# Second feed-forward block of a macaron block: its input half by Strassen's product with seven half-depth products, its output half in three chunks of rows

## The chip, the cores and the metric

The kernel runs on one core of one Trainium2 chip. The metric is the time of one execution on the device in microseconds (us). Three runs of the kernel before gave 2293.59, 2286.38 and 2290.88 us, so the median is 2290.88 us. One execution was profiled; all times of single instructions come from it.

## The reference

A block of a streaming encoder works on x with 1024 tokens of 1024 features:

```python
x = x + 0.5 * swiglu_ffn(rms_norm(x, ffn1_norm), ffn1_w_in, ffn1_w_out)
h = rms_norm(x, mix_norm)
...                                  # three mixers on h, merged by gates, times w_out, added to x
x = x + 0.5 * swiglu_ffn(rms_norm(x, ffn2_norm), ffn2_w_in, ffn2_w_out)
x = rms_norm(x, final_norm)

def swiglu_ffn(h, w_in, w_out):
    gate, up = split(h @ w_in, 2)    # w_in [1024, 2 * 2816], w_out [2816, 1024]
    return (silu(gate) * up) @ w_out
```

Only the second feed-forward block, the hand-over to it and the end of the kernel are touched by the change.

## The kernel before, in words

Every large product is computed from two fp16 parts of each operand, hi and lo, with three matmuls per 128 rows of depth: hi·hi, hi·lo and lo·hi (`matmul3`). A matmul has 128 output features on the partitions and 512 tokens, one half of the sequence, in its columns.

**Input half** (`ffn_in`). It has 22 tiles f. A tile is 128 gate columns and 128 up columns of w_in, for both halves of the tokens: 2 halves × 2 × 8 depths × 3 = 96 matmuls, 2112 for all. The gate's sum lies in PSUM as `mm`, the up one's as `lg`. ScalarE takes silu of the gate (`si`), and VectorE multiplies (`gt`). `Rows.put` then makes row f of the matrix for the output half: ScalarE squares `gt` for a sum, VectorE gets a power of two from it (`rsc`, `Hi`, `Hj`), ScalarE makes the hi part of `H` and VectorE the lo part.

**Weights** (`WBlock`). A block is loaded by a DMA (`wf`, two buffers), squared on ScalarE, summed over the partitions by a small matmul with ones (`ms`), turned into a scale on VectorE (`wsc`), and split: hi on ScalarE, lo on VectorE (`wh`, three buffers).

**Output half** (`out_stage`, blocks from `out_block`). There are 16 units: 8 tiles d of 128 output features by two halves. A unit is 22 rows × 3 = 66 matmuls: 60 for the first 20 rows in a bank `mm` (`begun`) and 6 for the last two rows in a bank `lg` (`ended`), since the scales of the weights' rows depend on the rows of H (`wrs`). VectorE adds both to x (`xo`, `xn`). In `final` the result is transposed, squared and normalized: on the last tile d = 7 a chain of twelve small operations on VectorE (`nv`, `ny`, `rsu`) gives 1/rms, and the 128x1024 tiles are scaled and stored. `tail_order` puts the last m tiles d half by half, here m = 2: (6,0), (7,0), (6,1), (7,1). The last unit comes in two pieces of 256 tokens.

**The hand-over.** The stage ahead multiplies the merged mixers by w_out. When a half of x is complete, `norm_split` scales it by 1/rms and the gain on VectorE (`hs<-xa,gs,lg`), copies hi on ScalarE (`xa<-hs`), and subtracts for lo on VectorE and GpSimd in turn (`xa<-hs,xa`). The input half begins with half 0 of two tiles, so 96 matmuls need nothing of half 1.

**What sets the order.** The program is written by generators under one clock model: `Model` estimates each engine's time, `Sched` lets the thread go on that is due, and `Stream.prep` emits the steps of the weight blocks ahead of their use when their engines are at most 3 us behind TensorE. Each engine then executes its own instructions in this order, waiting where an operand is not there. All instructions pass one helper, so the profile shows the line L61 for each, and groups are told apart by the tiles' names.

## Time and profile before

| | |
|---|---|
| median of three runs | 2290.88 us (2286.38 to 2293.59) |
| profiled execution, span | 2287.5 us |
| profiled execution's own time beside its span | not listed by itself; the runs' median is 3.4 us above the span |
| PE, DVE, ACT, POOL busy | 96%, 55%, 51%, 10% of the span |
| matmul instructions | 12604 |
| first product of the second input half | starts at 1574.53 us |
| first product of its output half | starts at 2039.92 us |

PE is TensorE, DVE VectorE, ACT ScalarE and POOL GpSimd. The busy shares are means over stages which differ: in the second feed-forward block GpSimd does nothing and the other two are busy for about a third of the time.

### The profile page before, as it was taken

The numbers are of one execution on the slowest core, as the hardware profiler recorded it, in microseconds if no ns is written. First come the engines' busy times: TensorE is split into PE (matmuls) and PEld (weight loads), VectorE is DVE, ScalarE is ACT, GpSimd is POOL, SyncE is SP. The second block draws the span as 40 slices with busy tenths as digits, with TensorE's granted clock in tenths as the row PEclk, the third lists the DMA queues.
The fourth block names the chain that finished last, engine by engine and source line by source line (L and its number), as shares of the span: only waits on it lengthen the run. The fifth ranks groups of instructions, "written<-read, shape, count | busy, mean of one in ns | idle before, by whom it ended". The sixth has DMA issues, their size and how long they took to land.

```text
span 2287.5 us, 33499 instructions
## 1 busy us (share of the span) xinstructions
PE 2192.5 (96%) x12604; PEld 1146.7 (50%) x12604; DVE 1258.8 (55%) x3818; ACT 1163.3 (51%) x2471; POOL 220.9 (10%) x463
## 2 busy tenths in 40 slices
PE   6999999999999889989999999899999999999998
PEld 3555444444444556575566764344444444444445
DVE  6446843244554477768569877667332233245553
ACT  6543434344443588778876766535343334344331
POOL 1201130000000013302200015401000000000000
PEclk9999999999999999989999999999999999999999
DMA  6422231202232111214322123353111111212212
GB/s 221 126 80 79 58 102 56 62 26 84 92 107 65 42 38 61 78 30 147 102 70 70 48 89 116 100 156 107 56 40 53 56 56 37 70 44 69 70 41 87
DMA packets 210866, 176.79 MB, mean 77 GB/s; under 512 B 7008, under 2 KB 187424, under 8 KB 210064
## 3 DMA queue, kind: packets, MB, share of 16 engines
q1 hardware_dynamic: 195008, 131.64, 18.4%
q0 software_dynamic: 8272, 28.84, 4.0%
q10 hardware_dynamic: 7424, 14.18, 2.1%
q8 instruction: 98, 1.61, 0.3%
q14 instruction: 64, 0.52, 0.1%
HBM read 139.38 MB, written 36.30 MB: 77 GB/s over the span
## 4 chain that ended last, share of the span: by engine, by line
PE 71%; DVE 13%; ACT 9%; issue 3%; POOL 2%; DMA 1%; DVEq 0%; ACTq 0%; POOLq 0%
PE mm L61 44%; PE lg L61 24%; ACT junk L61 3%; PE ms L61 3%; DVE at L61 2%; DVE wh L61 2%; DVE xa L61 1%; DVE dump L61 1%; PE ao L61 1%; ACT wh L61 1%; DVE wk L61 1%; DVE sb L61 1%; ACT mp L61 1%; POOL rsu L61 1%; DVE hs L61 1%
## 5 line engine op out<-in xcount | busy, mean ns | idle before, releaser
L61 PEld LDWEIGHTS <-wh 128*128 128x128 f16 x8418 | 816.5, 98 | 988.6 <-issue 35.9
L61 PE MATMUL mm<-xa,wh 128*128 128x512 f16 x3264 | 735.2, 380 | 6.4 <-ACT xa L61 4.9
L61 PE MATMUL lg<-xa,wh 128*128 128x512 f16 x2112 | 476.3, 380 | 0.0
L61 DVE SCALAR_TENSOR_TENSOR gt<-lg,wsc,si 128x512 f32<-128x512 f32 x88 | 66.0, 750 | 367.7 <-PE lg L61 346.7
L61 PE MATMUL mm<-H,wh 128*128 128x512 f16 (+1 forms) x1020 | 213.0, 366 | 0.0
L61 PE MATMUL mm<-G,wh 128*128 128x512 f16 x960 | 210.5, 379 | 0.0
L61 ACT ACTIVATE junk<-wf 128x128 f16<-128x128 f32 (+3 forms) x332 | 200.9, 605 | 17.9 <-DMA wf<-in_w_in_dram 10.5
L61 DVE SCALAR_TENSOR_TENSOR wh<-wf,wsc,wh 128x1024 f16<-128x1024 f32 (+1 forms) x132 | 166.1, 1261 | 56.5 <-ACT wh L61 56.4
L61 ACT ACTIVATE wh<-wf,wrs 128x128 f16<-128x128 f32 (+2 forms) x392 | 130.4, 403 | 103.9 <-DVE wrs L61 103.9
L61 ACT ACTIVATE si<-mm,wsc 128x512 f32<-128x512 f32 x88 | 59.7, 678 | 218.1 <-PE mm L61 207.6
L61 ACT ACTIVATE junk<-gt 128x1024 f16<-128x1024 f32 x44 | 46.5, 1056 | 237.7 <-DVE gt L61 237.7
L61 ACT ACTIVATE wh<-wf,wsc 128x1024 f16<-128x1024 f32 (+1 forms) x132 | 147.1, 1120 | 18.8 <-DVE wsc L61 17.2
L61 PE MATMUL mm<-wh,xa 128*128 128x256 f16 (+2 forms) x1152 | 130.8, 273 | 12.2 <-ACT us L61 6.6
L61 DVE SCALAR_TENSOR_TENSOR wh<-wf,wrs,wh 128x128 f16<-128x128 f32 (+2 forms) x392 | 124.8, 373 | 15.9 <-ACT wh L61 14.7
L61 PEld LDWEIGHTS <-xa 128*128 128x128 f16 x1152 | 108.7, 107 | 31.0 <-issue 13.8
L61 ACT ACTIVATE junk<-wk,kathr 128x1024 f16<-128x1024 f32 (+2 forms) x96 | 99.5, 1036 | 8.7 <-POOL kathr L61 6.8
L61 POOL TENSOR_TENSOR xa<-hs,xa 128x512 f16<-128x512 f32 x24 | 29.2, 1218 | 585.6 <-ACT xa L61 585.6
L61 DVE SCALAR_TENSOR_TENSOR xo<-mm,wsc,xo 128x512 f32<-128x512 f32 (+1 forms) x33 | 24.2, 734 | 92.2 <-PE mm L61 90.2
L61 ACT ACTIVATE sq<-xa 128x512 f32<-128x512 f32 x28 | 17.6, 629 | 109.0 <-DVE xa L61 105.7
L61 DVE TENSOR_SCALAR_CACHE_REDUCE dump<-wk,kt 128x384 f16<-128x384 f32 (+2 forms) x96 | 71.3, 743 | 2.0
L61 PE MATMUL mm<-m,wh 128*128 128x512 f16 x288 | 68.5, 393 | 3.7 <-DVE wh L61 3.2
L61 ACT ACTIVATE at<-at,asm,gac 128x128 f32<-128x128 f32 (+7 forms) x64 | 55.3, 865 | 27.3 <-DVE asm L61 26.9
(479 smaller groups left out, 2431.7 us busy)
## 6 DMA issues: line engine op xcount, KB each, us to landing
wf<-in_ffn_w_in_dram SPq DMA_DIRECT2D x88, 512.0 KB, 4.6
wf<-in_ffn_w_out_dram SPq DMA_DIRECT2D x16, 1280.0 KB, 6.0
gd<-gt SPq DMA_DIRECT2D x48, 256.0 KB, 2.0
xa<-gd POOLq DMA_DIRECT2D x16, 768.0 KB, 5.0
wf<-in_w_in_dram SPq DMA_DIRECT2D x17, 512.0 KB, 4.8
xo<-xd ACTq DMA_DIRECT2D x32, 256.0 KB, 2.6
xd<-xa SPq DMA_DIRECT2D x32, 256.0 KB, 2.4
wf<-in_w_in_dram SPq DMA_DIRECT2D x8, 1024.0 KB, 5.0
```

The lines of the kernel that those rows point to most:

```text
L61: r = f(*a, **k)
```

## The change

The product [gate; up] = w_inᵀ h is cut into 2 × 2 × 2: gate or up columns, the two halves of the depth, the two halves of the tokens. Strassen's product (in Winograd's form) then needs seven products of half the depth in place of eight. Per tile these are A11·B11, A12·B21, S1·T1, S2·T2, S3·T3, A22·T4 and S4·B22: 7 × 4 depths × 3 = 84 matmuls.

- **Sums of weights** (`SBlock`): four additions of 128x512 on GpSimd give S1 to S4 in one buffer `wsum`. Seven forms of 512 columns are split to hi and lo, in two buffers of the ring: A11, A12, S1, S2, and A22, S3, S4.
- **Sums of h** (`norm_forms` in place of `norm_split`): B11 and B21 from half 0 alone, then T2, T1, T3, T4 and B22, for which half 1 is needed; subtractions on VectorE and GpSimd, hi copies on ScalarE, lo on VectorE.
- **Sums of products** (`ffn_strassen`): ScalarE copies A11·B11 out of PSUM (`s["a"]`), VectorE makes five additions, each with one operand in PSUM, and GpSimd both products with silu. Their results lie in the place of x (names `xa` and `early`).
- **Output half**: rows 0 to 7 are multiplied after tile 8 of the input half, rows 8 to 14 after tile 15, rows 15 to 21 at the end. A chunk uses blocks of 256 columns. The first two chunks add to x in DRAM (`xd`): a unit reads its tile, VectorE adds, SyncE's queue writes it back. The last chunk is `out_stage` with `per` = 2 and m = 1.

```diff
+class SBlock(WBlock):
...
+        add = lambda o, x, y, op: nc.gpsimd.tensor_tensor(o, x, y, op=op)
+        if i == 0:
+            add(s1, self.a(2), self.a(3), OP.add)
+            add(s2, s1, self.a(0), OP.subtract)
+        else:
+            add(s3, self.a(0), self.a(2), OP.subtract)
+            add(s4, self.a(1), s2, OP.subtract)
...
+    def norm_forms(self, xa, half, sums, gi, name, F):
...
+        for k in range(K):
+            norm(k)
+            sub(nc.gpsimd, h(k, 0), h(k, 1), h(k, 0))
+            norm(k + K)
+            yield pace()
+        for k in range(K):
+            t2 = sp(self.t2("hs"))
+            sub(nc.vector, t2, h(k + K, 1), h(k, 0))
+            parts("T2", k, t2, nc.vector)
+            sub(nc.gpsimd, h(k + K, 0), h(k + K, 0), t2)
+            yield pace()
...
+                if form == "T3":
+                    sub(nc.gpsimd, h(k, 1), h(k + K, 1), h(k, 1))
+                parts(form, k, src(k), nc.vector)
...
+    def ffn_strassen(self, name, rows, a, b, F, ring, chunks, xd):
...
+            product(b2, w, "S2", "T2", False)
+            u2, u3 = ring(), ring()
+            nc.vector.tensor_tensor(u2, b2, s["a"], op=OP.add)
...
+            product(b3, w, "S1", "T1", False)
...
+            product(b2, w, "S3", "T3", True)
+            nc.vector.tensor_tensor(u3, b2, s["a"], op=OP.add)
...
+            nc.vector.tensor_tensor(c22, b3, u3, op=OP.add)
+            product(b4, w, "A22", "T4", False)
+            nc.vector.tensor_tensor(u3, b4, u3, op=OP.add)
+            gt = st[f] = ring("gt")
+            nc.gpsimd.tensor_tensor(gt[:, 0:HT], u3, s["si"], op=OP.mult)
...
+            product(b3, w, "S4", "B22", True)
+            w.use[1].uses -= 1
+            nc.vector.tensor_tensor(u2, b3, u2, op=OP.add)
+            nc.scalar.activation(u2, u2, AF.Silu, scale=w.inv)
+            nc.gpsimd.tensor_tensor(gt[:, HT:2 * HT], c22, u2, op=OP.mult)
...
+        yield f"h{name}.0"
+        for f in range(2):
+            yield from head1(f)
+        for f in range(2):
+            yield from head2(f)
+        for f in range(2):
+            yield from body(f, "f" + name + ".{}" if f == 0 else None, False)
+            put(f)
...
-    g1, g2 = Rows(kb, NF, "G"), Rows(kb, NF, "H")
+    chunks = [(0, 8), (8, 15), (15, 22)]
...
-            yield from kb.out_stage(b2, g2, xo, xd[2], 1, 2, done, cut=(0, HT // 2, HT), between=between)
+            yield from kb.out_stage(b2[-1], g2, xo, xd[2], 2, 1, done, cut=(0, HT // 2, HT), between=between)
```

The clock model orders the program anew, so the engines' orders move. On VectorE between two tiles of the input half, the order before is as follows (`wsc` the next weights' scale, `gt` the products with silu, `rsc` to `H` the row, `wh` the low parts of the next weights):

```order
L61 TENSOR_SCALAR wsc_18235<-wsc_18235,ginv_102 128x1
L61 SCALAR_TENSOR_TENSOR gt_18254<-lg_18185,wsc_17824,si_18255 128x512
L61 SCALAR_TENSOR_TENSOR gt_18254<-lg_18259,wsc_17824,si_18308 128x512
L61 TENSOR_SCALAR rsc_18311<-rsc_18311 128x1 x2
L61 TENSOR_SCALAR Hi_105<-rsc_18311 128x1
L61 TENSOR_TENSOR Hj_106<-Hi_105 128x1
L61 SCALAR_TENSOR_TENSOR H_18312<-gt_18254,rsc_18311,H_18312 128x1024
L61 SCALAR_TENSOR_TENSOR wh_18335<-wf_18201,wsc_18235,wh_18335 128x1024 x2
```

After the change the same place reads as follows (`xa<-lg` and `xa<-ao` are the additions of products; `wsum` holds S1 and S2 in the first of its splits, S3 and S4 in the second):

```order
L61 TENSOR_SCALAR wsc_17195<-wsc_17195,ginv_102 128x1
L61 TENSOR_TENSOR xa_91<-ao_17130,xa_91 128x512
L61 TENSOR_TENSOR xa_91<-lg_17202,xa_91 128x512
L61 SCALAR_TENSOR_TENSOR wh_17218<-wf_17009,wsc_17195,wh_17218 128x1024
L61 TENSOR_TENSOR xa_91<-ao_17130,xa_91 128x512
L61 SCALAR_TENSOR_TENSOR wh_17218<-wsum_17144,wsc_17195,wh_17218 128x1024
L61 TENSOR_SCALAR rsc_17238<-rsc_17238 128x1 x2
L61 TENSOR_SCALAR Hi_105<-rsc_17238,wsc_17057 128x1
L61 TENSOR_TENSOR Hj_106<-Hi_105 128x1
L61 SCALAR_TENSOR_TENSOR H_17239<-xa_91,rsc_17238,H_17239 128x1024
```

The low parts of S1 and S2 of the next tile now stand behind the last addition of this tile (`xa<-ao`), ahead of the row's chain; before, the next weights' low parts stood behind the row.

On VectorE at the hand-over, for half 1 of h, the order before is (a part of the eight pairs):

```order
L61 SCALAR_TENSOR_TENSOR hs_16316<-xa_91,gs_177,lg_16291 128x512
L61 SCALAR_TENSOR_TENSOR hs_16318<-xa_91,gs_177,lg_16291 128x512
L61 TENSOR_TENSOR xa_91<-hs_16316,xa_91 128x512
L61 SCALAR_TENSOR_TENSOR hs_16322<-xa_91,gs_177,lg_16291 128x512
L61 SCALAR_TENSOR_TENSOR hs_16326<-xa_91,gs_177,lg_16291 128x512
L61 TENSOR_TENSOR xa_91<-hs_16322,xa_91 128x512
L61 SCALAR_TENSOR_TENSOR hs_16330<-xa_91,gs_177,lg_16291 128x512
L61 SCALAR_TENSOR_TENSOR hs_16348<-xa_91,gs_177,lg_16291 128x512
```

After the change it is (`FT2`, `FT1` and `FT3` are the low parts of forms of h, `hs` the difference T2 itself, `early` a sum of products of the first tile):

```order
L61 SCALAR_TENSOR_TENSOR xa_91<-xa_91,gs_177,lg_16263 128x2x256 x8
L61 TENSOR_TENSOR hs_16307<-xa_91 128x512
L61 TENSOR_TENSOR FT2_15407<-hs_16307,FT2_15407 128x512
L61 TENSOR_TENSOR hs_16312<-xa_91 128x512
L61 TENSOR_TENSOR FT2_15407<-hs_16312,FT2_15407 128x512
L61 TENSOR_TENSOR hs_16317<-xa_91 128x512
L61 TENSOR_TENSOR FT2_15407<-hs_16317,FT2_15407 128x512
L61 TENSOR_TENSOR hs_16322<-xa_91 128x512
L61 TENSOR_TENSOR FT2_15407<-hs_16322,FT2_15407 128x512
L61 TENSOR_TENSOR FT1_15408<-xa_91,FT1_15408 128x512 x4
L61 TENSOR_TENSOR FT3_15409<-xa_91,FT3_15409 128x512
L61 TENSOR_TENSOR early_16352<-lg_16338,early_16201 128x512
```

All eight norms now come ahead of the first form, and five forms of four pieces follow them (T4 and B22 come behind the rows shown); before, each piece of h was ready for TensorE after its own norm and subtraction.

At the start of the last chunk of the output half, VectorE has after the change (`wrs` the scales of its rows 15 to 19, `H_20533` row 21):

```order
L61 TENSOR_TENSOR xa_91<-ao_20414,xa_91 128x512
L61 TENSOR_SCALAR wsc_20520<-ms_20521 128x1
L61 TENSOR_SCALAR wsc_20520<-wsc_20520 128x1 x2
L61 TENSOR_SCALAR wrs_20526<-Hi_105,wsc_20520 128x5
L61 SCALAR_TENSOR_TENSOR junk2_20530,wrq_20500<-wf_20428 128x256
L61 TENSOR_SCALAR rsc_20532<-rsc_20532 128x1 x2
L61 TENSOR_SCALAR Hi_105<-rsc_20532,wsc_20335 128x1
L61 TENSOR_TENSOR Hj_106<-Hi_105 128x1
L61 SCALAR_TENSOR_TENSOR H_20533<-xa_91,rsc_20532,H_20533 128x1024
L61 SCALAR_TENSOR_TENSOR wh_20546<-wf_20287,wrs_20526,wh_20546 128x256 x5
L61 SCALAR_TENSOR_TENSOR wj_20564,wss_20475<-wrq_20476,Hj_106 128x2
```

where before it had:

```order
L61 TENSOR_SCALAR wrs_19337<-Hi_105,wsc_19331 128x20
L61 SCALAR_TENSOR_TENSOR wh_19351<-wf_19056,wrs_19337,wh_19351 128x128 x8
L61 SCALAR_TENSOR_TENSOR gt_19305<-lg_19316,wsc_18783,si_19392 128x512
L61 TENSOR_SCALAR rsc_19395<-rsc_19395 128x1 x2
L61 TENSOR_SCALAR Hi_105<-rsc_19395 128x1
L61 TENSOR_TENSOR Hj_106<-Hi_105 128x1
L61 SCALAR_TENSOR_TENSOR H_19396<-gt_19305,rsc_19395,H_19396 128x1024
L61 SCALAR_TENSOR_TENSOR wh_19351<-wf_19056,wrs_19337,wh_19351 128x128 x4
```

Before, the first eight low parts of the output weights stood ahead of the last row's chain; now all five of the chunk's first block stand behind it.

## Rows read from the trace of the kernel before

**Rows 1.** The page: busy time and share of each engine, and two lines of the span in 40 slices (tenths busy; PEclk is TensorE's granted clock in tenths).

```profile
PE 2192.5 (96%) x12604; PEld 1146.7 (50%) x12604; DVE 1258.8 (55%) x3818; ACT 1163.3 (51%) x2471; POOL 220.9 (10%) x463
PE   6999999999999889989999999899999999999998
PEclk9999999999999999989999999999999999999999
```

**Rows 2.** Busy time of each engine in stretches (from:to, length, then PE, PEld, DVE, ACT, POOL busy with counts, then TensorE's granted clock, the DMA engines' share and GB/s).

```profile
1550.00:1574.00 24.00, 20.98 (x104) 10.07 (x103) 18.47 (x38) 11.19 (x17) 3.65 (x4) 1.00 0.33 100
1650.00:1700.00 50.00, 49.90 (x236) 22.70 (x235) 14.38 (x29) 16.55 (x25) 0.00 (x0) 1.00 0.22 64
2200.00:2250.00 50.00, 50.00 (x246) 24.02 (x245) 20.07 (x65) 11.02 (x37) 0.00 (x0) 1.00 0.06 17
```

**Rows 3.** The order of time (start, us, engine, operation): three half tiles of the input half and the start of the output half.

```profile
2014.00 5.34 PE L61 MATMUL lg<-xa,wh 128*128 128x512 f16 x24
2019.18 5.34 PE L61 MATMUL mm<-xa,wh 128*128 128x512 f16 x24
2024.36 5.34 PE L61 MATMUL lg<-xa,wh 128*128 128x512 f16 x24
...
2039.92 7.93 PE L61 MATMUL mm<-H,wh 128*128 128x512 f16 x36
```

**Rows 4.** Groups of instructions from 1600 to 2030 us, by tile and shape (count, busy us, mean ns, idle before).

```profile
L61 DVE SCALAR_TENSOR_TENSOR wh<-wf,wsc,wh 128x1024 f16<-128x1024 f32 x38 | 48.6, 1281 | 10.9 <-ACT wh L61 10.9
L61 ACT ACTIVATE wh<-wf,wsc 128x1024 f16<-128x1024 f32 x38 | 43.0, 1133 | 0.0
L61 ACT ACTIVATE junk<-wf 128x1024 f16<-128x1024 f32 x36 | 37.5, 1041 | 0.0
...
L61 ACT ACTIVATE si<-mm,wsc 128x512 f32<-128x512 f32 x42 | 28.4, 677 | 137.1 <-PE mm L61 137.1
L61 DVE SCALAR_TENSOR_TENSOR H<-gt,rsc,H 128x1024 f16<-128x1024 f32 x21 | 27.0, 1284 | 20.2 <-ACT H L61 20.2
...
L61 ACT ACTIVATE junk<-gt 128x1024 f16<-128x1024 f32 x21 | 22.2, 1056 | 111.9 <-DVE gt L61 111.9
```

**Rows 5.** Operations of 128x512 with both operands in SBUF on GpSimd and VectorE in the order of time, alone (the first two) and beside each other.

```profile
1362.04 1.26 POOL L61 TENSOR_TENSOR sb<-sb,sm 128x512 f32<-128x512 f32 x1 [7.12 <-DMA wf<-in_w_glu_dram]
1363.51 0.69 DVE L61 SCALAR_TENSOR_TENSOR xa<-xa 128x512 f32<-128x512 f32 x1 [1.55 <-ACT xa L61]
...
1377.54 1.28 DVE L61 SCALAR_TENSOR_TENSOR m<-xa,rsc,m 128x1024 f16<-128x1024 f32 x1
1377.72 2.23 POOL L61 TENSOR_TENSOR sb<-sb,sm 128x512 f32<-128x512 f32 x1 [4.86 <-DVE sm L61]
1378.74 1.76 DVE L61 SCALAR_TENSOR_TENSOR xa<-xa 128x512 f32<-128x512 f32 x1
```

**Rows 6.** The hand-over in the order of time: pieces of h for half 0, the first product, half 1's first pieces.

```profile
1566.32 1.29 ACT L61 ACTIVATE xa<-hs 128x512 f16<-128x512 f32 x2 [2.01 <-DVE hs L61]
1566.98 0.69 DVE L61 TENSOR_TENSOR xa<-hs,xa 128x512 f16<-128x512 f32 x1
...
1567.59 1.40 DVE L61 SCALAR_TENSOR_TENSOR hs<-xa,gs,lg 128x512 f32<-128x512 f32 x2
1567.69 1.16 POOL L61 TENSOR_TENSOR xa<-hs,xa 128x512 f16<-128x512 f32 x1 [84.83 <-ACT xa L61]
...
1574.53 0.82 PE L61 MATMUL mm<-xa,wh 128*128 128x512 f16 x3
...
1592.20 1.40 DVE L61 SCALAR_TENSOR_TENSOR hs<-xa,gs,lg 128x512 f32<-128x512 f32 x2
```

**Rows 7.** Short stretches around waits of TensorE, columns as in rows 2.

```profile
1579.00:1583.00 4.00, 1.75 (x14) 1.09 (x11) 2.41 (x5) 3.28 (x6) 0.00 (x0) 1.00 0.24 79
1583.00:1587.00 4.00, 4.00 (x14) 1.75 (x14) 3.02 (x13) 3.97 (x4) 0.00 (x0) 0.57 0.83 248
```

**Rows 8.** The last row's chain at the start of the output half, in the order of time.

```profile
2040.20 0.75 DVE L61 SCALAR_TENSOR_TENSOR gt<-lg,wsc,si 128x512 f32<-128x512 f32 x1 [4.35 <-PE lg L61]
...
2043.72 1.28 DVE L61 SCALAR_TENSOR_TENSOR H<-gt,rsc,H 128x1024 f16<-128x1024 f32 x1 [0.96 <-ACT H L61]
2044.92 1.13 DVE L61 SCALAR_TENSOR_TENSOR wh<-wf,wrs,wh 128x128 f16<-128x128 f32 x4
```

**Rows 9.** The end of the kernel in the order of time: the first rms chain's scalings, unit (6,1)'s last matmuls, the last unit in two pieces, the last rms chain.

```profile
2252.31 0.69 DVE L61 TENSOR_TENSOR xa<-lg,gb 128x512 f32<-128x512 f32 x1 [5.17 <-ACT junk L61]
...
2255.29 2.08 DVE L61 TENSOR_SCALAR xa<-xa,ny 128x1024 f32<-128x1024 f32 x3
...
2259.58 1.46 PE L61 MATMUL lg<-H,wh 128*128 128x512 f16 x6
2260.87 2.13 PE L61 MATMUL mm<-H,wh 128*128 128x256 f16 x18
...
2276.19 0.82 PE L61 MATMUL lg<-H,wh 128*128 128x256 f16 x6
...
2281.68 0.75 DVE L61 TENSOR_SCALAR xa<-xa,ny 128x1024 f32<-128x1024 f32 x1
```

## Prediction made before the changed kernel was run

> **What bounds the kernel now.** I read the page first, then the stretches, then the order of time at four places. TensorE is busy for 96% of the span at its full granted clock; GpSimd for 10% [rows 1]. By stretches the stages differ: around the hand-over TensorE works 21.0 of 24 us with VectorE busy for 18.5, while in the middle of the second feed-forward block it works 49.9 of 50 us in the input half and 50.0 in the output half, with VectorE and ScalarE busy for a third or less and GpSimd not at all [rows 2]. So matmuls taken from that block come off the end one for one, as long as no operand comes later than TensorE asks for it. The question is how many such waits the change makes.
>
> The sum is made against the profiled span, 2287.5 us; the median of the runs, 2290.88, is 3.4 above, and I add these at the end.
>
> **Term 1, the matmuls: −57.0.** A half tile of 24 matmuls starts 5.18 us after the one before (2014.00, 2019.18, 2024.36), so one takes 0.2158 us [rows 3]. Twelve fewer in each of 22 tiles are 264, worth 57.0 us. The output half has 1056 before and after: 8 + 7 + 7 rows are the same 22.
>
> **What lies beside them.** A tile now lasts 84 × 0.2158 = 18.1 us. VectorE has five additions of some 0.69, seven forms of low parts (3584 columns at 1.281 per 1024: 4.5), the row's low part 1.28 and small ones for about 1.4: 10.6. ScalarE has one copy and two silus (0.68 each), hi parts (3584 columns at 1.133 per 1024: 4.0), squares of weights about 2.5 (2 × 1.04 and the sums' reads), and the row (1.06 and about 1.3): some 10.9 [rows 4]. GpSimd's six operations at 1.2 make about 7.3 [rows 5]. None of the three fills the tile, so no engine becomes the bound by its load and this work costs nothing as long as the order suits. In the first two chunks a unit of 24 or 21 matmuls lasts 4.5 to 5.2 us; its addition on VectorE is 0.75 and its read and write of 256 KB lie behind TensorE, so I take 0 (upper end +4, should one read in each chunk come late).
>
> Where GpSimd and VectorE meet, rows 5 show a price: an operation of 1.26 on GpSimd took 2.23 and one of 0.69 on VectorE took 1.76 when both read two tiles in SBUF. In rows 6, where VectorE's operation has an operand in PSUM (`hs<-xa,gs,lg`, two in 1.40), it loses nothing beside GpSimd's 1.16. The Trainium skill, "SBUF — State Buffer", section "Who interferes with whom", says the same: a VectorE instruction with at most one SBUF input does not contend with GpSimd, one with two contends with its reads. By that rule a tile's five additions, each with an operand in PSUM, would pay nothing, and only splits and forms would; the trace agrees as far as it goes.
>
> **Term 2, the start of the input half: +29.** Count from the first product on h (1574.53 before). Before, 2112 matmuls took until 2039.92, 465.4 us, of which 455.8 are their own time [rows 3, 6]: 9.6 were waited. After the change only 48 matmuls (10.4 us) need nothing of half 1, in place of 96 (20.7). Half 1's norms begin on VectorE at about +15.5 (+17.7 before, 1592.20), and all eight come ahead of the first form: 8 × 0.70 gives +21.2. T2 is then four turns of a difference on VectorE, a copy on ScalarE (0.64) and a low part on VectorE, while GpSimd subtracts from the same tiles: 0.69 + 0.64 + 0.69 + about 0.05 without collision, 2.07; with GpSimd in the way, as in rows 5, I take 2.55, so +32 with the last landing. T1, between GpSimd's subtractions for T3, is there at +39; T3 at +42.5, T4 at +46, the splits of A22 and the sums at +48, B22 at +53, and S4·B22 ends at +56. The second tile's products take 13, wait 2.4 for the addition behind the first row's low part, and lose about 3 at the lower clock after the waits: both tiles' 168 matmuls end at about +74 and have 36.3 us of work, so 38 are waited, against 9.6: +29. Without collisions the same chain gives +17; with all of GpSimd's work held back, +34.
>
> **Term 3, low parts of S1 and S2 between tiles: +14.7.** In 14 of the tiles (4 to 8, 11 to 15, 18 to 21) VectorE has the next tile's low parts of S1 and S2 directly behind the last addition, and ScalarE has silu ahead of their hi parts. After S4·B22 ends: 0.11 for the signal, addition 0.69, silu 0.66, hi 1.13, low 1.28 [rows 4], and some 0.15 of signals: about 4.05. TensorE has the next tile's A11·B11 and two matmuls of S2·T2 meanwhile, 14 × 0.2158 = 3.02. Each tile waits 1.05. The ends: 0, if silu is issued behind the hi part in time or the addition's signal is quicker than that, and 2 per tile, if the split meets GpSimd's product with silu as in rows 5: 0 to +28.
>
> **Term 4, the starts of chunks 1 and 2: +7.** Their first block's scale waits for the row that precedes it, then a hi and a low part of 256 columns, before the third matmul: a gap of some 2.8 each. After a like gap before, TensorE works 1.75 of 4 us and then gets a clock of 0.57 for 4 us [rows 7], which loses 1.7. Of that I count half: 5.6 + 1.7. Ends 0 and 9.
>
> **Term 5, the last chunk's start: +8.3.** Before, the last row's chain, from the `gt` at 2040.20 to the end of its low part at 2045.00, lay behind 60 matmuls (12.9 us) of twenty rows whose low parts had been split already; the output half follows at 2039.92 without a gap [rows 3, 8]. Now only five rows precede, 15 matmuls (3.2 us), and VectorE has row 21's low part ahead of those rows' own splits. The third matmul is late by about 7 us, and a small wait of 1.3 for the last two rows' scale follows. Ends 4 and 11.
>
> **Term 6, the tail: +9.0.** Before, from the end of unit (6,1) at 2260.9 to 2287.5 are 26.6 us: two pieces of the last unit (66 matmuls of 256 columns each) until 2277.0, and 10.5 of chain behind them [rows 9]. With seven rows a last unit has 45 matmuls less, 9.7 us of term 1. But with m = 1 both rms chains now stand in this stretch, one behind the other on VectorE: unit (7,0) with its 21 matmuls, its transposes, four squares on ScalarE, the product 0.69, the chain of twelve operations and three scalings (2252.31 to 2257.37 is 5.1 us) is 12.8; the first piece adds 3.6 on VectorE; the last piece's own chain is about 9.5. That makes 25.9: of the 9.7 only 0.7 remain. Ends 5 and 10.
>
> **Term 7, waits for the last two rows' scales in two units of the last chunk: +2**, ends 0 and 5.
>
> The sum is −57.0 + 29 + 14.7 + 7 + 8.3 + 9.0 + 2 = +13.0. The span becomes 2300.5, and with 3.4 the time 2304. The ends of terms 2 to 7 give 17 + 0 + 0 + 4 + 5 + 0 = 26 and 34 + 28 + 9 + 11 + 10 + 5 + 4 = 101: −31 and +44 if all fell on one side. All on one side is unlikely; the forecast's own range is 2294 to 2315.
>
> **The rivals.** *A: GpSimd and VectorE do not get in each other's way* where term 2 says so. For it: the beside-each-other cases in rows 6 lose nothing. Against it: rows 5. Term 2 becomes 18 and term 3 loses 3: 2304 − 14 = 2290, no change. *B: the low parts of S1 and S2 arrive in time*, since the wait of term 3 is the difference of two numbers, 4.05 and 3.02, each known to a few tenths, and a silu that starts a step later removes it: 2304 − 14.7 = 2289, no change. *A and B together*: 2304 − 11 − 14.7 = 2278, faster. *C: the collisions go on through all tiles.* GpSimd's four sums and two products then meet VectorE's splits, the row's low part and with it the addition in front of S3 are late, and S3 waits: VectorE's 10.6 us grow by two collisions of 1.0 in each of 20 tiles, on a chain with slack 0.5 to 1.6. It decides from the point where the added delay exceeds this slack; at 2 us in 20 tiles the time is 2304 + 40 = 2344, clearly slower. For it: rows 5 show more than a doubling. Against it: additions with an operand in PSUM do not pay in rows 6. *D: the half-depth product does not save its matmuls* cannot be, as their number is in the program.
>
> **How the numbers follow.** Forecast 0.48, A 0.20, B 0.12, A and B 0.10, C 0.10. A measurement of this kernel can tell 0.3%, 6.9 us, from no change: faster is below 2284, slower above 2297.8. The forecast's case lies above that for most of its range (0.41 of 0.48) and within for the rest; A and B each have a fifth or so below 2284 and some above 2297.8, A with B is faster, C slower. That makes faster 0.18, same 0.28, slower 0.54. The range leaves out C and most of A with B: 2280 to 2321.
>
> **What would show it.** Term 2: on VectorE after the first products, eight norms, then T2 turns of 2.5 us, with TensorE waiting for `FT2`; the second row's products end 74 us after the first. Term 3: before the third matmul of S2·T2 a gap of 1 us in 14 tiles, its releaser VectorE's `wh<-wsum`. Term 5: about 7 us without matmuls behind the first two of the last chunk. Term 6: some 26 us from (6,1)'s last matmul to the end. In the middle of the input half TensorE at 94% of the time would fit term 3, 100% would be B, under 85% C. The prediction is wrong if the start costs under 15 or the tiles' waits lie elsewhere than at S2.

## The result, and the profile after

The changed kernel takes 2312.05 us, the median of four runs (2309.45 to 2312.88); the kernel before, on the same chip, 2290.61 (2286.38 to 2293.59). The ratio is 1.0094, 95% interval 1.0079 to 1.0108: slower by 0.9%. The forecast was 2304 in a range of 2280 to 2321. The profiled execution has a span of 2307.7 us, 20.2 longer than before.

The page, the line that answers to the first of [rows 1]:

```profile
PE 2151.3 (93%) x12291; PEld 1112.2 (48%) x12295; DVE 1374.5 (60%) x3796; ACT 1196.0 (52%) x2381; POOL 418.2 (18%) x603
```

TensorE is busy for 41 us less, 93% of the span in place of 96%; GpSimd for nearly twice as long. No other engine is anywhere near full, so the time is in waits. The view of waits (engine, what it waited for, us in total, times, longest), TensorE from 1540 us to the end:

```profile
PE lg L61 <- DVE wh L61: 11.4, 15, 0.8
PE mm L61 <- ACT wh L61: 11.0, 4, 6.0
PE lg L61 <- DVE xn L61: 9.7, 2, 5.5
PE lg L61 <- ACT FT L61: 5.3, 4, 4.6
```

Each of the forecast's terms has a line here: low parts of the weights between tiles (`lg <- DVE wh`), the chunks' first blocks (`mm <- ACT wh`), the tail (`lg <- DVE xn`), and the start (`FT`; a wait for `early` is in the next rows). The order of time at TensorE shows where (start, us, operation, in brackets the idle time before it and its releaser):

```profile
1579.58 2.75 PE L61 MATMUL mm<-FB,wh 128*128 128x512 f16 x12
...
1605.11 0.58 PE L61 MATMUL lg<-FT,wh 128*128 128x512 f16 x1 [4.59 <-ACT FT L61]
...
1631.40 4.44 PE L61 MATMUL ao<-FB,wh 128*128 128x512 f16 x12 [2.71 <-DVE early L61]
...
1651.21 2.75 PE L61 MATMUL mm<-FB,wh 128*128 128x512 f16 x12
...
1787.14 0.60 PE L61 MATMUL mm<-H,wh 128*128 128x512 f16 x2 [2.33 <-ACT wh L61]
...
2007.79 0.60 PE L61 MATMUL mm<-H,wh 128*128 128x512 f16 x2 [1.94 <-ACT wh L61]
...
2201.57 1.04 PE L61 MATMUL mm<-H,wh 128*128 128x512 f16 x2 [6.01 <-ACT wh L61]
...
2275.57 3.40 PE L61 MATMUL mm<-H,wh 128*128 128x512 f16 x15
```

The first product on h starts at 1579.58, both first tiles are done at 1651.21, the three chunks start behind gaps of 2.3, 1.9 and 6.0, and at 2275.57 unit (6,1) is done. Between such marks I take a stage's length less its own matmuls at 0.2158 us, after and before. What the lower clock costs behind a wait is in these lengths too. The differences add up to the span's:

| stage | forecast, us | measured, us |
|---|---|---|
| matmuls saved (term 1) | −57.0 | −57.0 |
| ahead of the block, in the mixers | 0 | +5.0 |
| start of the input half (term 2) | +29 | +25.8 |
| between tiles 2 to 21 (term 3) | +14.7 | +18.5 |
| starts of chunks 1 and 2 (term 4) | +7 | +7.7 |
| last chunk up to (6,1)'s end (terms 5 and 7) | +10.3 | +9.5 |
| tail behind it (term 6) | +9.0 | +10.7 |
| sum | +13.0 | +20.2 |

**One turn of T2** at the start, all engines:

```profile
1606.21 0.68 DVE L61 TENSOR_TENSOR hs<-xa 128x512 f32<-128x512 f32 x1
...
1606.92 0.63 ACT L61 ACTIVATE FT<-hs 128x512 f16<-128x512 f32 x1 [1.86 <-DVE hs L61]
1606.96 1.27 POOL L61 TENSOR_TENSOR xa<-xa,hs 128x512 f32<-128x512 f32 x1 [1.23 <-DVE hs L61]
1607.58 1.20 DVE L61 TENSOR_TENSOR FT<-hs,FT 128x512 f16<-128x512 f32 x1 [0.70 <-ACT FT L61]
1607.60 0.58 PE L61 MATMUL lg<-FT,wh 128*128 128x512 f16 x1 [0.25 <-ACT FT L61]
```

The difference, the hi copy, the low part, then the next turn: the next `FT` matmul comes at 1610.10, so a turn is 2.49 us. VectorE's low part takes 1.20 in place of 0.69, since GpSimd subtracts beside it.

**Between two tiles**, tile 3 to tile 4:

```profile
1687.77 0.69 DVE L61 TENSOR_TENSOR xa<-ao,xa 128x512 f32<-128x512 f32 x1 [0.71 <-PE ao L61]
1688.50 0.72 ACT L61 ACTIVATE xa<-xa,wsc 128x512 f32<-128x512 f32 x1 [3.83 <-DVE xa L61]
1689.12 1.13 ACT L61 ACTIVATE wh<-wsum,wsc 128x1024 f16<-128x1024 f32 x1
...
1690.29 1.35 DVE L61 SCALAR_TENSOR_TENSOR wh<-wsum,wsc,wh 128x1024 f16<-128x1024 f32 x1 [1.83 <-ACT wh L61]
1690.31 0.61 PE L61 MATMUL lg<-FT,wh 128*128 128x512 f16 x2
...
1691.70 1.47 PE L61 MATMUL lg<-FT,wh 128*128 128x512 f16 x6 [0.78 <-DVE wh L61]
```

This is the chain of term 3 with its own instructions: addition, silu, hi part, low part, then the third matmul of S2·T2. Tiles in which it stands last 19.3 us; tile 3, without it, 18.2.

**The tail**: VectorE between the first rms chain and the pieces of the last unit.

```profile
2288.19 2.08 DVE L61 TENSOR_SCALAR xa<-xa,ny 128x1024 f32<-128x1024 f32 x3
...
2290.78 0.48 DVE L61 SCALAR_TENSOR_TENSOR xn<-lg,wsc,xo 128x256 f32<-128x256 f32 x1
2291.41 0.66 PE L61 MATMUL lg<-ident,xn 128*128 128x128 f32 x2 [5.53 <-DVE xn L61]
...
2297.55 0.66 PE L61 MATMUL lg<-ident,xn 128*128 128x128 f32 x2 [4.20 <-DVE xn L61]
```

The first piece's matmuls were done at about 2284; its additions stand behind half 0's chain and scalings. The second piece's stand behind the first piece's own chain in the same way. From (6,1)'s end to the end of the span are 32.1 us, where [rows 9] show 26.6 before.

### The profile page after: what moved, and what is told of

Read it like the earlier page. It is cut to its first block, busy times and chain, and to the rows that moved or that the text cites. A ratio compares the mean times of both kernels' runs of the same rounds, so it can differ in the third digit from the quotient of the medians.

```text
span 2307.7 us, 33155 instructions
## 1 busy us (share of the span) xinstructions
PE 2151.3 (93%) x12291; PEld 1112.2 (48%) x12295; DVE 1374.5 (60%) x3796; ACT 1196.0 (52%) x2381; POOL 418.2 (18%) x603
## 4 chain that ended last, share of the span: by engine, by line
PE 64%; DVE 18%; ACT 11%; issue 4%; POOL 2%; DMA 1%; ACTq 0%; POOLq 0%; DVEq 0%; SPq 0%
PE mm L61 36%; PE lg L61 20%; PE ao L61 5%; ACT junk L61 4%; DVE wh L61 3%; PE ms L61 2%; DVE xa L61 2%; DVE at L61 2%; ACT wh L61 2%; DVE dump L61 1%; DVE FT L61 1%; DVE sb L61 1%; ACT xa L61 1%; DVE wk L61 1%; POOL xa L61 1%
## 5 line engine op out<-in xcount | busy, mean ns | idle before, releaser
L61 PE MATMUL mm<-xa,wh 128*128 128x512 f16 x2208 | 499.6, 381 | 6.5 <-ACT xa L61 4.9
L61 PE MATMUL lg<-xa,wh 128*128 128x512 f16 x1056 | 236.9, 379 | 0.0
L61 PE MATMUL mm<-H,wh 128*128 128x512 f16 (+1 forms) x975 | 214.6, 380 | 11.5 <-ACT wh L61 10.3
L61 PE MATMUL lg<-FT,wh 128*128 128x512 f16 x792 | 186.6, 385 | 23.8 <-DVE wh L61 11.0
L61 ACT ACTIVATE junk<-wf 128x1024 f16<-128x1024 f32 (+3 forms) x292 | 194.0, 664 | 19.0 <-DMA wf<-in_w_in_dram 10.3
L61 PE MATMUL mm<-wh,xa 128*128 128x256 f16 (+2 forms) x1152 | 131.0, 273 | 14.2 <-ACT us L61 7.8
L61 DVE SCALAR_TENSOR_TENSOR wh<-wf,wrs,wh 128x128 f16<-128x128 f32 (+2 forms) x304 | 114.5, 427 | 20.9 <-ACT wh L61 19.7
L61 PE MATMUL mm<-FB,wh 128*128 128x512 f16 x528 | 123.1, 383 | 3.5 <-DVE wh L61 2.8
L61 POOL TENSOR_TENSOR wsum<-wf 128x512 f32<-128x512 f32 x44 | 59.2, 1346 | 307.5 <-DMA wf<-in_ffn_w_in_dram 95.1
L61 DVE SCALAR_TENSOR_TENSOR gt<-lg,wsc,si 128x512 f32<-128x512 f32 x44 | 33.0, 749 | 129.1 <-PE lg L61 110.1
L61 POOL TENSOR_TENSOR xa<-xa 128x512 f32<-128x512 f32 x48 | 78.2, 1631 | 156.7 <-DVE xa L61 85.9
L61 POOL TENSOR_TENSOR xa<-hs,xa 128x512 f16<-128x512 f32 x16 | 19.9, 1248 | 476.8 <-ACT xa L61 476.8
L61 DVE TENSOR_TENSOR xa<-lg,xa 128x512 f32<-128x512 f32 x60 | 41.3, 688 | 93.7 <-PE ms L61 62.5
L61 DVE SCALAR_TENSOR_TENSOR wh<-wsum,wsc,wh 128x1024 f16<-128x1024 f32 x44 | 57.4, 1304 | 34.5 <-ACT wh L61 32.8
```

Of the source, the lines that this page charges most:

```text
L61: r = f(*a, **k)
```

## The experiments

My theory was the forecast's: an order of emission, not a full engine, costs terms 3, 5 and 6, and GpSimd beside VectorE costs part of term 2. The rivals were that collisions do nothing (A) or go on through all tiles (C). The stages ahead of the block, which no experiment touches, vary by up to 4 us between the traces (the first product on h starts between 1579.1 and 1583.3), so single stages are compared too.

**1. Both parts of S1 and S2 ahead of the tile's last product.**

```diff
...
+            if 2 <= f < NF - 1 and f not in (8, 15):
+                a[f + 1].go("s12")
             product(b3, w, "S4", "B22", True)
```

> Only the order changes: in tiles 2 to 20, where the next tile follows at once, the splits of the next tile's S1 and S2 (hi on ScalarE, lo on VectorE) are emitted ahead of S4 x B22, so ahead of the tile's last addition and its silu. If the waits at S2 x T2 come from that place in the order (a tile with the wait lasts 19.30 us, one without 18.18, the last of a chunk 19.9), they vanish in 14 tiles: 11 x 1.1 + 3 x 1.7 = 17 us less, a time of about 2295. Rival: VectorE's and GpSimd's work in the tiles is the bound, then the wait moves to S3 (behind the row's low part, now later) and less than 5 us are gained, about 2308.

Measured: 2307.92 us, ratio 1.0079 (1.0062 to 1.0096). A tile now lasts 19.06 us, 0.24 less. The wait at S2 is gone, and another has come three products later. In the order of time:

```profile
1685.59 1.27 DVE L61 SCALAR_TENSOR_TENSOR wh<-wf,wsc,wh 128x1024 f16<-128x1024 f32 x1
1685.81 2.17 POOL L61 TENSOR_TENSOR xa<-xa 128x512 f32<-128x512 f32 x1 [2.86 <-DVE xa L61]
1686.78 2.29 DVE L61 SCALAR_TENSOR_TENSOR wh<-wsum,wsc,wh 128x1024 f16<-128x1024 f32 x1
...
1688.99 0.68 DVE L61 TENSOR_TENSOR xa<-ao,xa 128x512 f32<-128x512 f32 x1
...
1697.87 0.68 DVE L61 TENSOR_TENSOR xa<-lg,xa 128x512 f32<-128x512 f32 x1
...
1698.61 1.67 PE L61 MATMUL lg<-FT,wh 128*128 128x512 f16 x7 [0.72 <-ACT xa L61]
```

The low part, moved ahead, meets GpSimd's product and takes 2.29; the tile's last addition stands behind it and starts at 1688.99, 1.6 after the next tile's first matmul (1687.37), where the changed kernel has 0.2 (1687.77 after 1687.57). The row's chain is later by about as much, and at its end `xa<-lg`, the addition that empties the bank which S3 writes. The profile names ScalarE's `xa` as the releaser, but the one that was under way there ended at 1698.62, when the matmul had begun; the addition ended at 1698.55, 0.06 ahead of it. So the order of emission was the reason, and moving both parts of the pair moved the wait.

**2. Only the hi part ahead; on VectorE the addition stays first.**

```diff
...
+            if ahead:
+                a[f + 1].hi()
             product(b3, w, "S4", "B22", True)
             w.use[1].uses -= 1
             nc.vector.tensor_tensor(u2, b3, u2, op=OP.add)
+            if ahead:
+                a[f + 1].go("s12")
             nc.scalar.activation(u2, u2, AF.Silu, scale=w.inv)
```

> Mends what the first try at S1 and S2 left: only the hi parts of the next tile's S1 and S2 go ahead of S4 x B22 on ScalarE; VectorE keeps the tile's last addition first and the low part behind it. In e1_s12_first the wait at S2 went, and one of 0.7 to 0.8 us came at S3, because the low part (2.29 us there, beside GpSimd's product) stood ahead of the last addition and put the row's chain off by 1.2 us. If the two waits are one chain, VectorE's order around the last addition, then with the addition first neither is left: tiles last 18.2 us (19.30 in the changed kernel, 19.06 in e1_s12_first), and the time falls by 15 to 17 us to about 2296. Rival: the tile is bound by the row's chain anyway: a tile stays above 18.8 us and the gain below 6 us.

Measured: 2297.86 us, ratio 1.0034 (1.0022 to 1.0047), 14.2 less than the changed kernel. The same place:

```profile
1691.78 0.69 DVE L61 TENSOR_TENSOR xa<-ao,xa 128x512 f32<-128x512 f32 x1 [0.71 <-PE ao L61]
1692.38 1.28 DVE L61 SCALAR_TENSOR_TENSOR wh<-wsum,wsc,wh 128x1024 f16<-128x1024 f32 x1
1692.50 0.72 ACT L61 ACTIVATE xa<-xa,wsc 128x512 f32<-128x512 f32 x1 [2.79 <-DVE xa L61]
...
1694.16 2.75 PE L61 MATMUL lg<-FT,wh 128*128 128x512 f16 x12
```

The low part follows the addition at once, beside silu and not behind it, and S2·T2 runs its twelve matmuls in one piece. Tiles 2 to 21 last 18.1 to 18.2 us, those before a chunk 18.4 to 18.5. So term 3 was ScalarE's order: between the tiles 16.6 us came back, and the median moved less because the first product on h came 3.7 later in the profiled execution.

**3. GpSimd's subtractions in the forms of h left out.**

```diff
-            sub(nc.gpsimd, h(k, 0), h(k, 1), h(k, 0))
...
-            sub(nc.gpsimd, h(k + K, 0), h(k + K, 0), t2)
...
-                    sub(nc.gpsimd, h(k, 1), h(k + K, 1), h(k, 1))
```

> Leaves out GpSimd's twelve subtractions in the forms of h (T1, T3 and T4 are then made from operands not subtracted). If GpSimd and VectorE get in each other's way there, a turn of T2 falls from 2.49 to about 2.07, T1's turns (1.67 each) to about 0.7, and the products of the first two tiles end 6 to 8 us earlier. Rival A: they do not: the turns of T2 stay at 2.5 and the end moves by less than 2 us.

Measured in one run: 2303.07 us, span 2301.3. VectorE's low part and two turns of T2 at TensorE:

```profile
1606.63 0.69 DVE L61 TENSOR_TENSOR FT<-hs,FT 128x512 f16<-128x512 f32 x1 [0.69 <-ACT FT L61]
1606.65 1.74 PE L61 MATMUL lg<-FT,wh 128*128 128x512 f16 x3 [0.25 <-ACT FT L61]
...
1608.64 1.74 PE L61 MATMUL lg<-FT,wh 128*128 128x512 f16 x3 [0.25 <-ACT FT L61]
```

The low part is back at 0.69, a turn lasts 1.99 in place of 2.49, and tile 2 starts at 1644.68, 6.5 us earlier than 1651.21. Four turns of T2 make 2.0 of these; T1's low parts, which stood beside GpSimd's subtractions for T3, follow each other at 0.60 in place of 1.67, which is most of the rest. So the collision at the start is real, worth 6.5 of term 2's 25.8; rival A falls.

**4. The products of tiles 0 and 1 by turns** (T2 of both, then T1 of both, and so on), so that TensorE has twice the work per form of h.

```diff
-        for f in range(2):
-            yield from body(f, "f" + name + ".{}" if f == 0 else None, False)
-            put(f)
+        yield from pair("f" + name + ".{}")
...
```

> The products of tiles 0 and 1 are taken in turns, form by form (S2 x T2 of both, S1 x T1 of both and so on), the second tile's S1 x T1 in a free bank. If the start costs what it does because TensorE has one tile's 12 matmuls for each form that VectorE makes, the second tile's 48 matmuls (10.4 us) and the wait of 2.4 us in it fall into the waits, three additions and a split come earlier on VectorE (about 2.7 us): both tiles end about 10 us earlier, a time of about 2302. Rival: the products of the second tile are not what the end waits for, since VectorE's additions for it and the first rows stand behind the forms: less than 3 us.

Measured: 2312.16 us, ratio 1.0097 (1.0082 to 1.0112). Both tiles are done 62.1 us after the first product, 9.5 earlier than the 71.6 of the changed kernel, and the time is the same. Tile 2 has it all back (its end comes 90.9 us after the first product, against 89.8):

```profile
1655.60 1.14 ACT L61 ACTIVATE wh<-wsum,wsc 128x1024 f16<-128x1024 f32 x1
...
1656.79 1.03 PE L61 MATMUL lg<-FT,wh 128*128 128x512 f16 x2 [7.67 <-ACT wh L61]
```

Both tiles end together, so two rows' chains stand on ScalarE in succession, and the hi part of tile 2's S1 and S2 behind both.

**5. Tail with m = 2**, the order of the kernel before.

```diff
-            yield from kb.out_stage(b2[-1], g2, xo, xd[2], 2, 1, done, cut=(0, HT // 2, HT), between=between)
+            yield from kb.out_stage(b2[-1], g2, xo, xd[2], 2, 2, done, cut=(0, HT // 2, HT), between=between)
```

> Only the order of the last chunk's units: m = 2, so (6,0), (7,0), (6,1), (7,1) as in the kernel before, in place of m = 1. If the tail is three chains of 1/rms one behind the other on VectorE (unit (7,0) until 2290.3, the first piece until 2296.4, the second until the end at 2307.7), the first of them begins one unit earlier, 5 us, and the end comes 3 to 5 us earlier: about 2308. Rival: TensorE's products and transposes are what the end waits for: no gain, 2312.

Measured: 2313.28 us, ratio 1.0099 (1.0084 to 1.0114): no gain. From tile 21's end to the end are 115.1 us, against 112.1.

```profile
2288.82 0.75 DVE L61 SCALAR_TENSOR_TENSOR xn<-lg,wsc,xo 128x512 f32<-128x512 f32 x1
...
2289.72 1.09 PE L61 MATMUL lg<-ident,xn 128*128 128x128 f32 x4 [5.42 <-DVE xn L61]
```

Counted from tile 21's end, half 0's chain comes 3.9 earlier (its scalings start after 88.9 us in place of 92.8), and now it is (6,1)'s `xn` that stands behind it, with the two pieces still to come. Here it counted what stands behind a chain on VectorE, not when the chain begins.

**6. The last unit whole, its transposes and both chains behind its additions.**

```diff
-            if late:
-                turn(*late.pop())
+            while late and (last or late[0][0] < ND - 1):
+                turn(*late.pop(0))
...
-            yield from kb.out_stage(b2[-1], g2, xo, xd[2], 2, 1, done, cut=(0, HT // 2, HT), between=between)
-            between()
+            yield from kb.out_stage(b2[-1], g2, xo, xd[2], 2, 1, done, cut=(0, HT), between=between)
+            between(True)
```

> Only the tail: the last unit comes whole, and both units' transposes and 1/rms chains are emitted behind the last unit's additions. m = 2 gained nothing, since there unit (6,1)'s addition stood behind the first chain on VectorE and TensorE waited for it (5.4 us). If the tail is VectorE's chains in series with additions queued between them, the three chains become two without a wait of TensorE between: from the end of (6,1)'s matmuls to the end 32.1 us now, 26 to 28 us then, a time of about 2307. Rival: the end is bound by the output's DMA and by what a chain itself takes: less than 2 us.

Measured: 2309.15 us, ratio 1.0082 (1.0067 to 1.0098). The two waits of 5.5 and 4.2 are gone; one of 0.4 is left. From (6,1)'s end (2277.07) to the end (2306.7) are 29.6 us in place of 32.1. That is above the 26 to 28 expected: of 9.7 us of waits only 2.5 came back. Two chains still follow one another on VectorE, and 6.4 us pass from the last scaling to the end, in which the output is stored.

**7. The last chunk's row splits ahead of tile 21's last product.**

```diff
+            if f == NF - 1:
+                b[-1][0].go(("split", 0))
             product(b3, w, "S4", "B22", True)
```

> Only the order at the last chunk's start: the five rows' splits are emitted ahead of the last tile's S4 x B22, so ahead of row 21's chain. The wait of 6.0 us ahead of the chunk's first matmul goes, and a wait of 4 to 5 us comes ahead of the last two rows' matmuls, since row 21's chain (7 us) has 15 matmuls (3.2 us) to hide behind. Gain 3 to 4 us between the last tile and unit (0,0)'s end. Rival: the whole wait moves there, no gain.

Measured in one run: 2316.36 us, span 2314.6. The wait of 6.0 at the chunk's first matmul is gone, but from tile 21's end to the end are 115.9 us, 3.8 more, and tile 21 itself lasts 20.9 in place of 19.9. VectorE and TensorE up to the last two rows' scale (`ms`):

```profile
2197.94 2.08 DVE L61 SCALAR_TENSOR_TENSOR wh<-wf,wrs,wh 128x256 f16<-128x256 f32 x5 [0.58 <-ACT wh L61]
...
2199.93 0.68 DVE L61 TENSOR_TENSOR xa<-ao,xa 128x512 f32<-128x512 f32 x1
...
2208.70 0.75 DVE L61 SCALAR_TENSOR_TENSOR xo<-mm,wsc,xo 128x512 f32<-128x512 f32 x1 [1.86 <-DMA xo<-xd]
...
2209.58 0.16 PE L61 MATMUL ms<-wss,ones_b 128*128 128x1 bf16 x1 [7.64 <-DVE wj L61]
```

`wj`, the sum for the scale, stands behind the first unit's addition, which now comes ahead of it and waits for its load from DRAM, issued behind the row on ScalarE's queue. Row 21's chain is late as well: its first link, the tile's last addition at 2199.93, stands behind the five low parts that were moved ahead. This is the order that experiment 1 ran into.

**8. Edits 2, 4, 6 and 7 together**, with the hi and low parts of tile 2's S1 and S2 ahead of the first two rows' chains (the answer to experiment 4):

```diff
                 nc.vector.tensor_tensor(u2[i], b3[i], u2[i], op=OP.add)
+                if i == 0:
+                    a[2].go("s12")
                 nc.scalar.activation(u2[i], u2[i], AF.Silu, scale=w.inv)
```

> Together: e1b_hi_first, the two first tiles by turns (as e7_two_tiles, with tile 2's S1 and S2 split ahead of both rows' chains, whose wait of 7.7 us ate the 9.7 us that the turns gained), e8b_split_early and e2x_tail_whole. If these four places are what the change lost, 16 + 6 + 3.5 + 5 = 30 us less than the changed kernel, about 2281, faster than the kernel before by 0.4%. Rival: the waits go on to the next place in the chain: above 2291.

Measured: 2292.58 us, ratio 1.0012 (1.0003 to 1.0021). That is the rival's time, not the 2281 expected. From the first product on h to tile 2's end are 85.3 us, against 89.8 in the changed kernel; tile 2 still lasts 23.4. The tiles behind it have their full gain, but the last stage (tile 21's end to the end) is 115.2 us, longer than the 112.1 of the changed kernel.

**9. The same without edit 7.**

```diff
-            if f == NF - 1:
-                b[-1][0].go(("split", 0))
```

> The first combination (hi parts ahead, products of tiles 0 and 1 by turns, last unit whole) without its fourth part, the last chunk's row splits ahead of tile 21's last product. Theory (those splits cost 3.8 us in their own run, because the last two rows' scale comes to stand behind an addition that waits for its load): 3.5 to 4.5 us below the combination of four, 2288 to 2289, with the 6.0 us wait at the last chunk's first matmul back and no 8 us wait at 'ms'. Rival (the parts take the same time from each other, so a part that is harmful alone is harmless in company): 2292 to 2293.

Measured: 2289.64 us, ratio 0.9993 (0.9985 to 1.0002). The last stage is 112.5 us against 115.2: edit 7 costs in company what it cost alone, as the theory had it, if about 1 us less.

**10. Edit 7 again, with the first addend loaded ahead.**

```diff
                 b[-1][0].go(("split", 0))
+                self.pre()
...
+            def pre():
+                t = ready[0, 0] = kb.t2("xo")
+                nc.scalar.dma_start(t, xd[2][0, 0])
...
```

> All four parts, and the first addend of the last chunk (xo from xd) loaded where the splits are moved to, ahead of tile 21's last product, so that the addition ahead of the last two rows' scale finds it there. Theory (only this load made the splits late): the 8.3 us wait at 'ms' falls under 1.5 us and the 6.0 us wait at the first matmul stays away, so 5 to 6 us less than without the splits and about 9 less than the first combination: 2283 (2281 to 2285), below the kernel before by 0.2 to 0.4%. Rival (the addition also waits for its matmuls, and the row's low part stands ahead of it on VectorE anyway): a wait of 3 to 5 us stays at 'ms', and the time is that of the combination without the splits, 2288.

Measured: 2290.11 us, ratio 0.9995 (0.9986 to 1.0004). The last stage is 112.4 us, 2.8 less than with edit 7 alone, and no less than without it. The rival holds:

```profile
2185.30 1.29 DVE L61 SCALAR_TENSOR_TENSOR H<-xa,rsc,H 128x1024 f16<-128x1024 f32 x1 [0.97 <-ACT H L61]
2186.50 0.75 DVE L61 SCALAR_TENSOR_TENSOR xo<-mm,wsc,xo 128x512 f32<-128x512 f32 x1
...
2187.37 0.16 PE L61 MATMUL ms<-wss,ones_b 128*128 128x1 bf16 x1 [6.17 <-DVE wj L61]
```

The load is no longer waited for; row 21's own chain is, whose low part `H` ends at 2186.59. It takes 9.8 us from tile 21's last matmul to `ms`. About 2 us of these come from the edit itself: the five low parts stand ahead of the tile's last addition again, which starts at 2179.68, 2.1 after tile 21's matmuls end (in the changed kernel at once, 2195.59 after 2195.55). Hi parts alone ahead, as in experiment 2, were not tried here.

**11. Two units' long parts in front of these two rows.**

```diff
-            yield from kb.out_stage(b2[-1], g2, xo, xd[2], 2, 1, done, cut=(0, HT), between=between, ready=ready)
+            yield from kb.out_stage(b2[-1], g2, xo, xd[2], 2, 1, done, 2, cut=(0, HT), between=between, ready=ready)
```

> The last combination, and in the last chunk the long part of two units (30 matmuls) ahead of the first unit's last two rows, in place of one unit's (15 matmuls). Theory (what those two rows wait for is the row's own chain of tile 21: 9.8 us from tile 21's last matmul to 'ms' in the last run, of which 15 matmuls cover 5.7; 30 cover 11.4): the wait of 6.2 us at 'ms' falls to 1 to 1.5 us, which the second unit's addition, now ahead of the scale, sets; 4 to 6 us less, span 2284 to 2286, time 2284 to 2286, below the kernel before by 0.2 to 0.3%. Rival (the wait moves to the second unit's scale or to the end, whose chains set the time whatever stands ahead): waits of 5 us or more turn up behind it and the time stays at 2289 to 2291.

Measured: 2289.12 us, ratio 0.9995 (0.9986 to 1.0004): the rival's time, and the last stage is 112.4 us once more.

```profile
2173.26 6.74 PE L61 MATMUL mm<-H,wh 128*128 128x512 f16 x30
...
2184.20 0.75 DVE L61 SCALAR_TENSOR_TENSOR xo<-mm,wsc,xo 128x512 f32<-128x512 f32 x1 [1.06 <-DMA xo<-xd]
...
2185.08 0.16 PE L61 MATMUL ms<-wss,ones_b 128*128 128x1 bf16 x1 [5.09 <-DVE wj L61]
```

My expectation was mis-sized: I counted a matmul at 0.379 us, the duration which the trace gives one, where they start 0.216 apart. Thirty cover 6.5 us, not 11.4. The second addition with its load also came ahead of `wj`, so `ms` followed tile 21's end by 12.0 us in place of 9.8.

**12. The weights' sums on VectorE in place of GpSimd.**

```diff
-        add = lambda o, x, y, op: nc.gpsimd.tensor_tensor(o, x, y, op=op)
+        add = lambda o, x, y, op: nc.vector.tensor_tensor(o, x, y, op=op)
...
```

The clock model's entry for these sums is moved to VectorE with them.

> One part of the change undone: the weights' sums on VectorE in place of GpSimd (22 tiles x 4 sums; VectorE's additions of this size take 0.69 us, GpSimd's 1.26 to 1.40), all else as in the changed kernel. Theory (the wait at S2 is an order of emission, as the run with hi parts ahead showed, and beside GpSimd only single VectorE instructions grow): tiles 2 to 21 stay at 19.0 to 19.5 us, time 2308 to 2314. Rival 1 (the sums on GpSimd slow VectorE's low parts, 2.29 for 1.28 us, and so make the wait): tiles at 18.4 or less, time 2296 to 2300. Rival 2 (GpSimd carries work that VectorE has no room for, 22 x 2.76 = 61 us more): tiles over 20 us, time over 2325.

Measured: 2363.88 us, ratio 1.0318 (1.0302 to 1.0334). Counted from first matmul to first matmul, ten of the tiles 2 to 21 last 18.2 to 19.8 us, about as in the changed kernel; the other ten, in pairs, last 22.7 to 25.9. One of the waits between two of these:

```profile
1719.94 1.03 PE L61 MATMUL mm<-FB,wh 128*128 128x512 f16 x2 [3.19 <-ACT wh L61]
```

On VectorE two sums (1714.75 to 1717.11) stand ahead of the next scale (1717.29) and of this tile's last addition (1717.41); on ScalarE silu follows that addition and the next hi part follows silu. The size is rival 2's, the mechanism only in part: VectorE is busy for 61% of the span, so it is not out of room; the sums delay a chain in some tiles. GpSimd is the right place for them in this order, and they are not what term 3 paid for.

## Why the prediction was right, and where it was not

The direction and the mechanism were right: 57 us of matmuls saved, more than that paid in waits for operands. The time missed by 8 us (2304 against 2312): 7.2 of them in the span, the rest since the changed kernel's median lies 4.4 above its profiled span and not 3.4.

- **Term 1** held: matmuls of tiles without waits start 0.216 apart, and such a tile lasts 18.2 us.
- **Term 2** was 29 and is 25.8. Norms, then T2 turns of 2.49 (2.55 forecast), both tiles after 71.6 us (74). The lower clock behind the waits was sized well: 24 matmuls from 1621.73 take 6.94 us and 12 from 1631.40 take 4.44, where others take 5.34 and 2.75, so 3.3 are lost (3 forecast). Collisions are 6.5 of the term (experiment 3), where the forecast had 11 between its own case and A. So "with GpSimd in the way" was too dear, and the chain without it, 18 (17 in term 2 itself), too cheap by 1.3.
- **Term 3** was 14.7 and is 18.5. Both links named, silu ahead of the hi part and the low part behind it, are in the trace, and experiment 2 removed the wait by moving the first alone. The size was off: 1.12 per tile and not 1.05 in eleven tiles, and 1.7 in the three before a chunk, where TensorE waits for the hi part too.
- **Term 4** (7 against 7.7) held, and its half of a lost clock came out by chance. The two starts cost 4.7 and 3.0 with gaps that differ by 0.4 only: behind the first gap TensorE's granted clock falls to the lower of its two levels, 1.2 GHz (0.50 from 1789 to 1792), behind the second it stays at 2.4 (1.00 from 2008 to 2011). In experiment 5's trace the same two gaps have it the other way round, 3.0 and 4.7; in experiment 2's both cost 4.7.
- **Terms 5 and 7** (10.3 against 9.5) held in size, and in cause but for the place. The forecast put the wait behind the first two matmuls, at VectorE's low parts. It stands ahead of the first (6.0, and 0.36 behind the two), since row 21's hi part stands ahead of these rows' hi parts on ScalarE as its low part does on VectorE:

```profile
2199.96 1.15 ACT L61 ACTIVATE H<-xa,rsc 128x1024 f16<-128x1024 f32 x1 [0.41 <-DVE rsc L61]
...
2201.02 2.09 ACT L61 ACTIVATE wh<-wf,wrs 128x256 f16<-128x256 f32 x5
```

Experiments 7, 10 and 11 removed this wait and met row 21's chain a few matmuls later. They gained nothing, but they also delayed that chain themselves; what the chunk's start costs with the chain undelayed is open.
- **Term 6** was 9.0 and is 10.7, and this is two errors that nearly cancel. "With seven rows a last unit has 45 matmuls less, 9.7 us of term 1" is wrong for the stretch: behind (6,1) stand 42 matmuls of full width in place of 66, 24 fewer, 5.2 us. By that count the chain of 25.9 would have given +4.5. The chain is 32.1 us long, 6.2 more: 14.7 up to the end of the first scalings (2290.27) where I had 12.8, and 17.4 for the two pieces where I had 13.1. I had not put the additions of the last unit's pieces behind the rms chains on VectorE, and both are there; experiment 6 took them from there and got 2.5 back. That the term came within 1.7 is luck.
- **Left out**: +5.0 in the mixers, code that the diff does not touch. In every trace of the changed kernel and its variants the first product on h starts later than in the one trace of the kernel before, by 4.6 to 8.8, so this is hardly scatter alone. The one clock model orders the whole program, so the order there moved too. The waits there, the kernel before:

```profile
PE mm L61 <- ACT gc L61: 9.8, 6, 2.6
```

and the changed one:

```profile
PE mm L61 <- ACT gc L61: 15.5, 7, 3.7
```

That this wait is the 5.0, less what others got shorter, is argued from these lines and was not tried.

**The rivals.** A fell by experiment 3. B fell with the wait between tiles in the trace; its remedy worked when made (experiment 2). C fell: without the wait at S2 tiles last 18.2 us with all of GpSimd's sums in place.

**Where the gain of 57 stays.** The best version, experiment 11, has the kernel before's time within what can be measured. Its span of 2285.5 is 22.2 below that of the changed kernel: 6.2 less from the first product on h to tile 2's end, 16.6 less between the tiles behind it, and 0.6 more in the other stages together. Against the kernel before that leaves 19.7 at the start, 20.3 from the last chunk on, 7.4 at the two chunk starts, 5.8 in the mixers, 1.8 between tiles: 55.0 of 57.0. What the tiles lost can be had back by order, as experiment 2 shows. The start and the end are chains through VectorE and ScalarE with few matmuls beside them; that no order shortens them further is not shown. None of the versions beat the kernel before.

## What to carry to other kernels

Cutting matmuls from a stage that TensorE fills pays only while each operand's chain is shorter than the matmuls left beside it: write that chain down at every seam (first operands, between tiles, first rows, last unit), since the waits, with the lower clock behind them, cost 77 us here and the matmuls saved were 57. When two engines make an operand in turn, look first at what stands ahead of the first one; a silu ahead of a hi part cost 14 us, and moving both parts in place of one moved the wait instead of removing it. Count matmuls by the distance of their starts, and count at the tail what is behind the mark, not what the whole stage lost.

## What was not expected of the hardware

When VectorE and GpSimd meet with both operands in SBUF, the one that comes second seems to stand still until the other is done, and then takes about its own time. In experiment 1 VectorE's low part ends at 1686.86 and GpSimd's product, begun at 1685.81, ends 1.12 later (1.26 alone [rows 5]); the next low part, begun at 1686.78, ends 1.09 behind that product's end at 1687.98 (1.28 alone [rows 4]). In the T2 turn above the low part ends 0.55 behind GpSimd's end (0.69 alone), and the two collisions of [rows 5] read the same way: 1.13 and 0.55 behind the other's end. So the price is what is left of the other's instruction, which a forecast can read off the order, in place of the factor that I took from [rows 5]. The Trainium skill, "SBUF — State Buffer", section "Who interferes with whom", calls the ports that the two share an exclusive lock; these ends agree with it. Additions with an operand in PSUM kept 0.67 to 0.69 throughout: 110 in the changed kernel from 1575 to 2210, 47 of them beside a GpSimd instruction.
